# Whole first loads, a cut-up last tile and an early output in a row-wise cosine similarity

The chip is one Trainium2; the kernel runs on one of its cores. The metric is the device time of one execution in microseconds (us), as the median over several executions. All runs told here are fast (one core, granted clock 1.0).

## The reference

```python
x, y: float32 [8192, 8192]
x_norm = np.linalg.norm(x, axis=1, keepdims=True)
y_norm = np.linalg.norm(y, axis=1, keepdims=True)
return np.sum(x * y, axis=1) / (x_norm.squeeze() * y_norm.squeeze() + 1e-8)
```

For each of 8192 rows: the product of x and y summed, and the two sums of squares. Two inputs of 268 MB each are read once; 32 KB are written.

## The kernel before

64 tiles of 128 rows. Each tile is 4 MB of x and 4 MB of y. VectorE (DVE) makes the sum of x*y in one pass over 8192 columns, ScalarE (ACT) the two sums of squares in one pass each. (In the profile's lines PE is TensorE, and SPq is the queue of SyncE, which issues the loads.) Two buffers for x, two for y. The first tile's loads are cut into four groups of 32 rows.

```python
for r in range(0, P, 32):
    nc.sync.dma_start(out=xtiles[0][r : r + 32, :], in_=xv[0, r : r + 32, :])
    nc.sync.dma_start(out=ytiles[0][r : r + 32, :], in_=yv[0, r : r + 32, :])
nc.sync.dma_start(out=xtiles[1], in_=xv[1])
nc.sync.dma_start(out=ytiles[1], in_=yv[1])
# ... (identity, accumulators)
for t in range(n_tiles):
    sx = sqpool.tile([P, n_cols], bf16, tag="sq")          # one buffer
    if t + 2 < n_tiles:
        nc.sync.dma_start(out=xtiles[t + 2], in_=xv[t + 2])
        nc.sync.dma_start(out=ytiles[t + 2], in_=yv[t + 2])
    nc.vector.tensor_tensor_reduce(out=prod_s, in0=xt, in1=yt, ..., accum_out=xy_acc[:, t : t + 1])
    nc.scalar.activation(out=sx, in_=xt, func=Square, accum_out=xx_acc[:, t : t + 1])
    nc.scalar.activation(out=sx, in_=yt, func=Square, accum_out=yy_acc[:, t : t + 1])
# the short chain, once, over all 64 columns:
# nn = xx*yy (DVE), den = sqrt(nn) (ACT), rcp = 1/den (DVE), res = xy*rcp (DVE),
# transpose (PE), copy out of PSUM (DVE), one output of 64 rows of 128 values
```

## Time and profile before

| | before |
|---|---|
| median time | 1285.09 us (4 runs, 1284.73 to 1285.24) |
| span of the profiled run | 1283.3 us |
| y of tile 0 / tile 1 / tile 62 / tile 63 has landed | 43.7 / 63.0 / 1250.1 / 1269.55 us |
| from the last landing to the end of the span | 13.75 us |

The span runs from the first instruction to the last; the measured time is 1.8 us more. Landings are read off as the moment just before the pass that waited for the load, or from the chain in order of time. The profile's own lines are in the prediction below, each with what it says.

### The profile page before, as it was taken

Reading aid. Unit: us, or ns where it says so; the run is one execution under the profiler, and the core shown is the slowest. Engines: PE = TensorE matmul, PEld = TensorE weight load, DVE = VectorE, ACT = ScalarE, POOL = GpSimd, SP = SyncE. Lnnn points to the kernel's source line nnn. Section 1 sums busy time; section 2 is a strip of 40 time slices with the busy share of each in tenths; the row PEclk is TensorE's granted clock in tenths of the full one; section 3 lists DMA queues with packets and bytes.
Section 4 is the critical chain, followed back from the end, with each engine's and each line's share of the span. In section 5 each row is a group of like instructions: output and inputs, shape, how many; then the busy total and the mean of one; then the engine's idle time right before and its main releaser. Section 6 shows DMA issues by size and latency. Waiting matters only on the chain.

```text
span 1283.3 us, 905 instructions
## 1 busy us (share of the span) xinstructions
PE 0.4 (0%) x1; PEld 0.1 (0%) x1; DVE 558.0 (43%) x132; ACT 914.9 (71%) x261; POOL 0.7 (0%) x6
## 2 busy tenths in 40 slices
PE   0000000000000000000000000000000000000000
PEld 0000000000000000000000000000000000000000
DVE  0354354354353453453443543543544534534535
ACT  0677677777767767777776776777777677777766
POOL 0000000000000000000000000000000000000000
DMA  9999999999999999999999999999999999999994
GB/s 200 355 429 437 426 440 425 432 433 429 437 426 436 429 430 434 429 437 427 436 429 430 435 428 437 427 433 432 431 435 426 437 427 432 434 430 435 426 436 206
DMA packets 18615, 536.97 MB, mean 418 GB/s; under 512 B 2160, under 2 KB 2224, under 8 KB 2224
## 3 DMA queue, kind: packets, MB, share of 16 engines
q1 hardware_dynamic: 18608, 536.91, 98.9%
q14 instruction: 7, 0.06, 0.0%
HBM read 536.87 MB, written 0.03 MB: 418 GB/s over the span
## 4 chain that ended last, share of the span: by engine, by line
DMA 76%; DVE 22%; SPq 1%; issue 1%; DVEq 0%; PE 0%; ACT 0%
DMA yt<-in_y_dram 76%; DVE prod_s L74 22%; SPq L72 1%; DVEq L74 0%; DVE xy_acc L74 0%; DVE rcp L102 0%; SPq L73 0%; PE res_t_ps L107 0%; SPq L49 0%; DVE res_t L110 0%; ACT den L100 0%; DVE res L104 0%; DVE nn L98 0%
## 5 line engine op out<-in xcount | busy, mean ns | idle before, releaser
L74 DVE CUSTOM_DVE_ANT_0 prod_s<-xt,yt 128x8192 bf16<-128x8192 f32 x64 | 556.3, 8693 | 721.6 <-DMA yt<-in_y_dram 721.6
L84 ACT ACTIVATE sx<-xt 128x8192 bf16<-128x8192 f32 x64 | 449.9, 7029 | 197.8 <-DMA xt<-in_x_dram 197.8
L90 ACT ACTIVATE sx<-yt 128x8192 bf16<-128x8192 f32 x64 | 449.9, 7030 | 163.5 <-DMA yt<-in_y_dram 163.5
L90 ACT ACTIVATION_READ_ACCUMULATOR sx<-yt 128x1 f32 x64 | 11.9, 187 | 0.0
L84 ACT ACTIVATION_READ_ACCUMULATOR sx<-xt 128x1 f32 x64 | 11.9, 186 | 0.0
L74 DVE DVE_READ_ACCUMULATOR2_ANT xy_acc<- 128x1 f32 x64 | 5.3, 83 | 0.0
L55 ACT ACT_TABLE_LOAD x1 | 1.3, 1283 | 0.7 <-PEq L127 0.7
L100 ACT ACTIVATE den<-nn 128x64 f32<-128x64 f32 x1 | 0.3, 256 | 1.8 <-DVE nn L98 1.8
L56 ACT ACT_TABLE_LOAD x1 | 1.3, 1283 | 0.0
L107 PE MATMUL res_t_ps<-ident,res 128*64 128x128 f32 x1 | 0.4, 394 | 1279.8 <-DVE res L104 1279.8
L102 DVE RECIPROCAL rcp<-den 128x64 f32<-128x64 f32 x1 | 0.6, 552 | 0.3 <-ACT den L100 0.3
L110 DVE COPY res_t<-res_t_ps 64x128 f32<-64x128 f32 x1 | 0.3, 283 | 0.6 <-PE res_t_ps L107 0.6
masks.py:199 POOL TENSOR_SCALAR_AFFINE_SELECT ident<-ident 128x128 f32<-128x128 f32 x1 | 0.3, 292 | 0.1
L107 PEld LDWEIGHTS res_t_ps<-ident,res 128*64 128x64 f32 x1 | 0.1, 129 | 1279.8 <-issue 1279.8
L104 DVE TENSOR_TENSOR res<-xy_acc,rcp 128x64 f32<-128x64 f32 x1 | 0.2, 224 | 0.0
L98 DVE TENSOR_TENSOR nn<-xx_acc,yy_acc 128x64 f32<-128x64 f32 x1 | 0.2, 221 | 0.0
L55 ACT ACTIVATE dummy<-dummy 128x1 uint32<-128x1 uint32 x1 | 0.2, 203 | 0.0
L56 ACT ACTIVATE dummy<-dummy 128x1 f32<-128x1 f32 x1 | 0.2, 203 | 0.0
masks.py:197 POOL MEMSET ident<- 128x128 f32 x1 | 0.2, 204 | 0.3 <-POOLq L127 0.3
L127 POOL MEMSET const-bfloat16-1.0<- 128x1 bf16 x1 | 0.1, 101 | 0.0
L127 POOL MEMSET const-uint8-127<- 128x1 uint8 x1 | 0.1, 101 | 0.0
L127 POOL MEMSET const-float32-0.0<- 128x1 f32 x1 | 0.1, 98 | 0.2 <-issue 0.2
(1 smaller groups left out, 0.1 us busy)
## 6 DMA issues: line engine op xcount, KB each, us to landing
xt<-in_x_dram SPq DMA_DIRECT2D x63, 4096.0 KB, 20.2
yt<-in_y_dram SPq DMA_DIRECT2D x63, 4096.0 KB, 29.5
xt<-in_x_dram SPq DMA_DIRECT2D x4, 1024.0 KB, 21.3
yt<-in_y_dram SPq DMA_DIRECT2D x4, 1024.0 KB, 25.8
out_dram<-res_t SPq DMA_DIRECT2D x1, 32.0 KB, 1.8
```

The costliest lines, as they stand in the source:

```text
L55: nc.scalar.memzero(dummy)
L56: nc.scalar.sqrt(out=dummy, in_=dummy)
L72: nc.sync.dma_start(out=xtiles[t + 2], in_=xv[t + 2])
L74: nc.vector.tensor_tensor_reduce(out=prod_s, in0=xt, in1=yt, scale=1.0, scalar=0.0, op0=mybir.AluOpType.mult, op1=mybir.AluOpType.add, acc ...
L84: nc.scalar.activation(out=sx, in_=xt, func=mybir.ActivationFunctionType.Square, accum_out=xx_acc[:, t : t + 1],)
L90: nc.scalar.activation(out=sx, in_=yt, func=mybir.ActivationFunctionType.Square, accum_out=yy_acc[:, t : t + 1],)
L98: nc.vector.tensor_tensor(out=nn, in0=xx_acc, in1=yy_acc, op=mybir.AluOpType.mult)
L100: nc.scalar.activation(out=den, in_=nn, func=mybir.ActivationFunctionType.Sqrt)
L102: nc.vector.reciprocal(out=rcp, in_=den)
L107: nc.tensor.transpose(out=res_t_ps, in_=res, identity=ident)
L110: nc.vector.tensor_copy(out=res_t, in_=res_t_ps)
L127: nc = _bacc.Bacc("TRN2", target_bir_lowering=False, num_devices=1)
```

## The change

Its visible intent is a shorter end. The last tile's loads are cut by columns, so that work on a part can start before the rest has come; tiles 0 to 62 get their short chain and output while tile 63 is still loading; and the last tile's sums are arranged so that only a square root stands between its last square and the reciprocal. Along with it, without comment, the 32-row split of the first tile's loads goes. The diff is abridged, and its comments are mine:

```diff
-    for r in range(0, P, 32):
-        nc.sync.dma_start(out=xtiles[0][r : r + 32, :], in_=xv[0, r : r + 32, :])
-        nc.sync.dma_start(out=ytiles[0][r : r + 32, :], in_=yv[0, r : r + 32, :])
+    last = n_tiles - 1
+    XB = [0, 4096, 8192]
+    YB = [0, 1664, 3328, 4992, 6656, 8192]
+    cuts = {last: (XB, YB), last - 1: ([0, n_cols], [0, n_cols // 2, n_cols])}
+    # issue_dma(t): one load for each piece of cuts, else one whole load
+    issue_dma(0)
+    issue_dma(1)
 ...
+    for t in range(n_tiles - 1):
+        if t + 2 < n_tiles:
+            issue_dma(t + 2)
+        compute_tile(t)                      # as before; y of tile 62 in two passes and a sum
+        if t == n_tiles - 2:
+            chain(columns 0 to 62)           # the short chain and an output of 63 rows
+    squares(xt, XB, xxp)                     # one ACT pass a part, each with its own partial sum
+    total(xxp, nxc, xx_acc[:, lcol], "junkx")
+    squares(yt, YB[:-1], yyp)
+    total(yyp, nyc - 1, bias, "junky", scale=xx_acc[:, lcol])   # bias = xx * (y parts so far)
+    squares(yt[:, YB[-2]:], [0, n_cols - YB[-2]], yyp[:, nyc - 1:nyc])
+    # DVE: five parts of x*y, each starting from the sum of the part before (scalar=xyp[...])
+    nc.scalar.activation(out=den[:, lcol], in_=yyp[:, nyc - 1:nyc], func=Sqrt,
+                         scale=xx_acc[:, lcol], bias=bias)
+    # reciprocal, product, transpose, copy, output of one row of 128 values
```

More of the change, by code (lines that the diff above doesn't have):

```diff
@@ L46, with issue_dma, squares, total @@
     ]
-    for r in range(0, P, 32):
-        nc.sync.dma_start(out=xtiles[0][r : r + 32, :], in_=xv[0, r : r + 32, :])
-        nc.sync.dma_start(out=ytiles[0][r : r + 32, :], in_=yv[0, r : r + 32, :])
-    nc.sync.dma_start(out=xtiles[1], in_=xv[1])
-    nc.sync.dma_start(out=ytiles[1], in_=yv[1])
+    last = n_tiles - 1
+    XB = [0, 4096, 8192]
+    YB = [0, 1664, 3328, 4992, 6656, 8192]
+    cuts = {last: (XB, YB), last - 1: ([0, n_cols], [0, n_cols // 2, n_cols])}
+    def issue_dma(t):
+        xb, yb = cuts.get(t, ([0, n_cols], [0, n_cols]))
+        for a, b in zip(xb, xb[1:]):
+            nc.sync.dma_start(out=xtiles[t][:, a:b], in_=xv[t, :, a:b])
+        for a, b in zip(yb, yb[1:]):
+            nc.sync.dma_start(out=ytiles[t][:, a:b], in_=yv[t, :, a:b])
+    def squares(src, bounds, parts):
+        for c, (a, b) in enumerate(zip(bounds, bounds[1:])):
+            nc.scalar.activation(
+                out=sq_s[:, a:b], in_=src[:, a:b],
+                func=mybir.ActivationFunctionType.Square,
+                accum_out=parts[:, c:c + 1],
+            )
+    def total(parts, n, to, name, **kw):
+        junk = finpool.tile([P, n], fp32, tag=name)
+        nc.scalar.activation(
+            out=junk, in_=parts[:, 0:n],
+            func=mybir.ActivationFunctionType.Identity, accum_out=to, **kw,
+        )
+    issue_dma(0)
+    issue_dma(1)
     dummy = finpool.tile([P, 1], fp32, tag="dummy")
@@ L65, with compute_tile @@
     prod_s = prodpool.tile([P, n_cols], bf16, tag="prod")
-    for t in range(n_tiles):
+    sq_s = sqpool.tile([P, n_cols], bf16, tag="sq")
+    res = finpool.tile([P, n_tiles], fp32, tag="res")
+    nn = finpool.tile([P, n_tiles], fp32, tag="nn")
+    den = finpool.tile([P, n_tiles], fp32, tag="den")
+    rcp = finpool.tile([P, n_tiles], fp32, tag="rcp")
+    res_t_ps = psumpool.tile([n_tiles, P], fp32, tag="res_t_ps")
+    res_t = finpool.tile([n_tiles, P], fp32, tag="res_t")
+    res_t_ps_last = psumpool.tile([1, P], fp32, tag="res_t_ps_last")
+    res_row_last = finpool.tile([1, P], fp32, tag="res_row_last")
+    out_v = out.rearrange("(t p) -> t p", p=P)
+    def compute_tile(t):
         xt = xtiles[t]
         yt = ytiles[t]
-        sx = sqpool.tile([P, n_cols], bf16, tag="sq")
-        if t + 2 < n_tiles:
-            nc.sync.dma_start(out=xtiles[t + 2], in_=xv[t + 2])
-            nc.sync.dma_start(out=ytiles[t + 2], in_=yv[t + 2])
         nc.vector.tensor_tensor_reduce(
@@ L81 @@
             op1=mybir.AluOpType.add,
-            accum_out=xy_acc[:, t : t + 1],
+            accum_out=xy_acc[:, t:t + 1],
         )
         nc.scalar.activation(
-            out=sx,
+            out=sq_s,
             in_=xt,
             func=mybir.ActivationFunctionType.Square,
-            accum_out=xx_acc[:, t : t + 1],
+            accum_out=xx_acc[:, t:t + 1],
+        )
+        if t == last - 1:
+            yyp62 = accpool.tile([P, 2], fp32, tag="yyp62")
+            squares(yt, cuts[t][1], yyp62)
+            total(yyp62, 2, yy_acc[:, t:t + 1], "junk62")
+            return
@@ L89, with chain @@
+        nc.scalar.activation(
+            out=sq_s,
+            in_=yt,
+            func=mybir.ActivationFunctionType.Square,
+            accum_out=yy_acc[:, t:t + 1],
+        )
+    def chain(cols, ps, sb, orows):
+        nc.vector.tensor_tensor(
+            out=nn[:, cols], in0=xx_acc[:, cols], in1=yy_acc[:, cols],
+            op=mybir.AluOpType.mult,
         )
         nc.scalar.activation(
-            out=sx,
-            in_=yt,
-            func=mybir.ActivationFunctionType.Square,
@@ L94 @@
-            accum_out=yy_acc[:, t : t + 1],
-        )
-    nn = finpool.tile([P, n_tiles], fp32, tag="nn")
-    nc.vector.tensor_tensor(out=nn, in0=xx_acc, in1=yy_acc, op=mybir.AluOpType.mult)
-    den = finpool.tile([P, n_tiles], fp32, tag="den")
-    nc.scalar.activation(out=den, in_=nn, func=mybir.ActivationFunctionType.Sqrt)
-    rcp = finpool.tile([P, n_tiles], fp32, tag="rcp")
-    nc.vector.reciprocal(out=rcp, in_=den)
-    res = finpool.tile([P, n_tiles], fp32, tag="res")
-    nc.vector.tensor_tensor(out=res, in0=xy_acc, in1=rcp, op=mybir.AluOpType.mult)
@@ L106 @@
-    res_t_ps = psumpool.tile([n_tiles, P], fp32, tag="res_t_ps")
-    nc.tensor.transpose(out=res_t_ps, in_=res, identity=ident)
-    res_t = finpool.tile([n_tiles, P], fp32, tag="res_t")
-    nc.vector.tensor_copy(out=res_t, in_=res_t_ps)
-    out_v = out.rearrange("(t p) -> t p", p=P)
-    nc.sync.dma_start(out=out_v, in_=res_t)
+            out=den[:, cols], in_=nn[:, cols],
+            func=mybir.ActivationFunctionType.Sqrt,
+        )
+        nc.vector.reciprocal(out=rcp[:, cols], in_=den[:, cols])
@@ new lines, in chain @@
+        nc.vector.tensor_tensor(
+            out=res[:, cols], in0=xy_acc[:, cols], in1=rcp[:, cols],
+            op=mybir.AluOpType.mult,
+        )
+        nc.tensor.transpose(out=ps, in_=res[:, cols], identity=ident)
+        nc.vector.tensor_copy(out=sb, in_=ps)
+        nc.sync.dma_start(out=out_v[orows, :], in_=sb)
+    for t in range(n_tiles - 1):
[3 more added lines that the diff above has]
+        if t == n_tiles - 2:
+            e = slice(0, last)
+            chain(e, res_t_ps[e, :], res_t[e, :], e)
@@ new lines @@
+    lcol = slice(last, last + 1)
+    xt = xtiles[last]
+    yt = ytiles[last]
+    nxc, nyc = len(XB) - 1, len(YB) - 1
+    xxp = accpool.tile([P, nxc], fp32, tag="xxp")
+    yyp = accpool.tile([P, nyc], fp32, tag="yyp")
+    xyp = accpool.tile([P, nyc], fp32, tag="xyp")
+    bias = finpool.tile([P, 1], fp32, tag="bias")
+    squares(xt, XB, xxp)
[3 more added lines that the diff above has]
+    squares(yt[:, YB[-2]:], [0, n_cols - YB[-2]], yyp[:, nyc - 1:nyc])
@@ new lines @@
+    for c, (a, b) in enumerate(zip(YB, YB[1:])):
+        nc.vector.tensor_tensor_reduce(
+            out=prod_s[:, a:b], in0=xt[:, a:b], in1=yt[:, a:b],
+            scale=1.0,
+            scalar=0.0 if c == 0 else xyp[:, c - 1:c],
+            op0=mybir.AluOpType.mult, op1=mybir.AluOpType.add,
+            accum_out=xyp[:, c:c + 1],
+        )
+    nc.scalar.activation(
+        out=den[:, lcol],
+        in_=yyp[:, nyc - 1:nyc],
+        func=mybir.ActivationFunctionType.Sqrt,
+        scale=xx_acc[:, lcol],
+        bias=bias,
+    )
@@ L116 @@
+    nc.vector.reciprocal(out=rcp[:, lcol], in_=den[:, lcol])
+    nc.vector.tensor_tensor(
+        out=res[:, lcol], in0=xyp[:, nyc - 1:nyc], in1=rcp[:, lcol],
+        op=mybir.AluOpType.mult,
+    )
+    nc.tensor.transpose(out=res_t_ps_last[0:1, :], in_=res[:, lcol], identity=ident)
+    nc.vector.tensor_copy(out=res_row_last[0:1, :], in_=res_t_ps_last[0:1, :])
+    nc.sync.dma_start(out=out_v[last:last + 1, :], in_=res_row_last[0:1, :])
 _INS = ['x', 'y']
```

## The prediction

> **What bounds the kernel now.** I read the busy table and the slices of the page first, then the stretches of the head, then the timeline of the last 30 us, then the DMA issues.
>
> Page, busy table and slices:
>
> ```profile
> PE 0.4 (0%) x1; PEld 0.1 (0%) x1; DVE 558.0 (43%) x132; ACT 914.9 (71%) x261; POOL 0.7 (0%) x6
> ...
> DMA  9999999999999999999999999999999999999994
> GB/s 200 355 429 437 426 440 425 432 433 429 437 426 436 429 430 434 429 437 427 436 429 430 435 428 437 427 433 432 431 435 426 437 427 432 434 430 435 426 436 206
> ```
>
> No engine is near full, while the DMA row is 9 from start to end. But the GB/s row shows two slices that differ: the first (32 us) moves 200 GB/s with its DMA engines just as busy as later, and the second 355. The last, with 206, holds the end, where the loads are over. Those two places are where time can be had; in between nothing can, because the input is 536.87 MB and the rate is flat at about 431.
>
> Stretches (first column the stretch in us, second its length, last column GB/s, before it the DMA share):
>
> ```profile
> 0.00:3.20 3.20, 0.00 (x0) 0.00 (x0) 0.00 (x0) 2.43 (x3) 0.70 (x6) 1.00 0.69 164
> 3.20:43.80 40.60, 0.00 (x0) 0.00 (x0) 0.00 (x0) 5.45 (x3) 0.00 (x0) 1.00 0.99 207
> 43.80:63.00 19.20, 0.00 (x0) 0.00 (x0) 8.70 (x2) 16.45 (x6) 0.00 (x0) 1.00 1.02 437
> 63.00:1269.00 1206.00, 0.00 (x0) 0.00 (x0) 539.42 (x124) 883.20 (x248) 0.00 (x0) 1.00 1.00 431
> ```
>
> Until 43.8 us, while the eight 32-row loads of the first tile are under way, the same busy DMA engines move 207 GB/s; the first whole-tile loads after them move 437. The 32-row split halves the rate of its 8.39 MB.
>
> Timeline of the end (start, duration, engine, line, work, wait before it):
>
> ```profile
> 1250.22 7.03 ACT L90 ACTIVATE sx<-yt 128x8192 bf16<-128x8192 f32 x1 [2.58 <-DMA yt<-in_y_dram]
> 1259.94 7.03 ACT L84 ACTIVATE sx<-xt 128x8192 bf16<-128x8192 f32 x1 [2.60 <-DMA xt<-in_x_dram]
> 1266.87 0.19 ACT L84 ACTIVATION_READ_ACCUMULATOR sx<-xt 128x1 f32 x1
> 1269.63 7.03 ACT L90 ACTIVATE sx<-yt 128x8192 bf16<-128x8192 f32 x1 [2.58 <-DMA yt<-in_y_dram]
> 1269.71 8.69 DVE L74 CUSTOM_DVE_ANT_0 prod_s<-xt,yt 128x8192 bf16<-128x8192 f32 x1 [10.71 <-DMA yt<-in_y_dram]
> 1278.33 0.22 DVE L98 TENSOR_TENSOR nn<-xx_acc,yy_acc 128x64 f32<-128x64 f32 x1
> 1278.58 0.26 ACT L100 ACTIVATE den<-nn 128x64 f32<-128x64 f32 x1 [1.83 <-DVE nn L98]
> 1278.87 0.55 DVE L102 RECIPROCAL rcp<-den 128x64 f32<-128x64 f32 x1 [0.32 <-ACT den L100]
> 1279.46 0.22 DVE L104 TENSOR_TENSOR res<-xy_acc,rcp 128x64 f32<-128x64 f32 x1
> 1280.26 0.28 DVE L110 COPY res_t<-res_t_ps 64x128 f32<-64x128 f32 x1 [0.58 <-PE res_t_ps L107]
> 1280.57 0.55 SPq L112 DMA_DIRECT2D out_dram<-res_t  x1
> ```
>
> The last y has landed just before 1269.6 (I take 1269.55, from the chain in order of time). Then 13.75 us pass to the end of the span at 1283.3: 8.86 until the DVE has read its 8192 columns, 4.89 for the short chain and the output. The wait of 2.6 us before every ACT pass shows that ACT keeps pace with 9.7 us per 4 MB load; ACT and DVE bind only at the end.
>
> [...]
>
> **The change, part by part.**
>
> *Head: the 32-row split goes (not the visible aim of the change).* All first loads now span 128 partitions. Before, y of tile 1 lands at 63.02 (the chain: 13.43 + 49.59). After: first issue at 0.74; a fixed latency F; two tiles at full rate. The time of one tile at full rate is (1269.55 - 63.02) / 62 = 19.46 us. F from the first quarter: its load is 7.5 us from issue to landing, and 1.049 MB at 207 GB/s take 5.07, so F = 2.45. Hence y of tile 1 lands at 0.74 + 2.45 + 38.92 = 42.1. Gain 20.9 us. It is carried on to the end undiminished, as everything after is a queue at full rate: x of tile 2 is issued when DVE is done with tile 0, 8.8 us after y of tile 0 has landed, while tile 1 still has 10.6 us to transfer. Two loads are then always in flight, as before.
>
> *Middle.* Tiles 1 to 61 are unchanged: same work, same buffers. One sq buffer outside the loop instead of one of a pool with one buffer: the same. 0.
>
> *End: the loads of tile 63 are cut* into x 2 x 4096 columns and y 4 x 1664 + 1536, and tiles 0 to 62 get their chain and output early. I count from the landing of y of tile 62 as zero (before: 1250.14, so the end of the span is +33.16). A column takes 19.46/16384 us to load: x parts land at 4.87 and 9.73, y parts at 11.7, 13.7, 15.7, 17.6, 19.46.
> DVE: tile 62 until 8.7; early chain until about 11, in gaps; each y part costs 1664/0.96 ns + 0.16 fixed (8.69 less 8192/0.96 ns) = 1.9, with its accumulator read and semaphore some 2.0, the same as the arrival. So DVE ends at 19.5 + 1.76 + about 0.3 = 21.5.
> ACT: one pass costs its columns x 0.833 plus 0.32 fixed (from start to next start 7.15 us for 8192 columns, trace at 38.89 to 46.04). The second x half lands at 9.73, start 9.81, 3.73 -> 13.54. Then ACT is behind and never waits again: four y parts of 1.71 each = 6.84; the sum of the x parts 0.35; the sum of four y parts with a pointer scale 0.5; the last y part 1.60. Total 9.29 -> 22.83. So **ACT, not DVE or the DMA, ends the tail**, 3.4 us after the last landing, because it has the 3.4 us of x half to catch up on.
> Then: sqrt with pointer scale and bias 0.45 -> 23.3; reciprocal of one column about 0.2 (0.55 for 64) -> 23.5; product 0.25 -> 23.75; transpose 0.55 with its wait -> 24.3; copy 0.3 -> 24.6; output from end of copy to end of span 2.76 as before -> 27.35.
> 33.16 - 27.35 = 5.8 us gained. The small added instructions before it (early chain, its 63-row output, the two-part sum) lie beside the loads.
>
> *Sum:* 1285.09 - 20.9 - 5.8 = **1258.4 us**, 2.1% less.
>
> **Rivals.**
> A. The head gains nothing: the slow first 44 us are a start-up effect of memory, not of the 32 rows. For it: I infer the cause from position alone, the 32-row loads and the start fall together. Against: the rate is constant at 207 over four quarters and jumps at once to 437 with the first 128-row load, no warming up[...]. Then 1285.09 - 5.8 = 1279.3.
> B. The narrow column loads run slower (rows of 6.7 and 16 KB instead of 32 KB) or the queue has gaps between them. [...] As ACT is behind anyway in y, most of this is hidden; at most 1259.
> C. The tail gains less, as ACT pays more per part: self-waits on the partial sums, an extra table load. The built program has two table loads, both at the start, as before, so no switch of 1.28 us; 0.1 us more on each of nine instructions would give 1259.3. On the other side, if ACT kept up with the loads, DVE would be last and the time 1257.
> D. Buffers: the last parts' issues wait for earlier loads to land before they may be issued. The built order shows the fourth y part waiting for x of tile 62, the fifth for the first half of y of tile 62. Both have landed well before those parts' turn (about -9.7 and -4.9 on my clock, turn at 15.7 and 17.6), so 0. Were it wrong, the queue would empty for a few us: 1261.
>
> **Range and chances.** The head term is uncertain by about 0.6 us (F was measured at half the rate), the tail by 0.8, the rate over 62 tiles by 0.3 (the four runs lie 0.5 apart); A is unlikely. 1258.4, with 1256.4 to 1260.4 for 8 in 10. The 2% line is 1259.4, only 1 us away, so: faster by over 2% 0.77, within 2% 0.22, slower 0.01.
>
> **What would show it.** Right: the first slice of GB/s near 400, the first ACT pass starting near 13 us instead of 38.89, the second y landing near 42; flat 431 in between; at the end ACT without idle time from the second x half to the last square, DVE idle a little before each of its last parts, the last square ending 3 to 3.5 us after the last landing. Wrong: the first DVE pass still near 44 us (rival A), a hole in the DMA row in the last two tiles (D), or DVE's last product ending after ACT's last square (the tail worked out wrongly).

## The result, and the profile after

| | before | after |
|---|---|---|
| median time | 1285.10 us (13 runs, 1284.73 to 1285.35) | 1256.34 us (8 runs, 1256.19 to 1256.52) |
| span of the profiled run | 1283.3 us | 1254.6 us |
| y of tile 1 has landed | 63.02 us | 42.23 us |
| from the landing of y of tile 62 to the end | 33.2 us | 25.3 us |

The ratio is 0.9776 (95% interval 0.9767 to 0.9786): faster by over 2%. A ratio is the mean time of one kernel's fast runs over that of the other's of the same rounds, so not quite the ratio of the medians. The predicted 1258.4 is 2.06 us too high, and the measured median lies 0.06 us below the range.

The slices of the changed kernel's page (busy tenths of the DMA engines, then GB/s):

```profile
DMA  9999999999999999999999999999999999999997
GB/s 401 435 435 434 434 426 429 434 435 434 434 426 430 433 434 434 434 429 427 434 434 434 433 428 429 434 434 433 434 428 429 434 433 434 433 428 427 435 429 312
```

The first slice has gone from 200 GB/s to 401, the second from 355 to 435. The DMA row could not have told: it was 9 both times. The stretches of the changed kernel (stretch, length, busy time of PE, its weight loads, DVE, ACT, POOL, clock, DMA share, GB/s):

```profile
0.00:3.00 3.00, 0.00 (x0) 0.00 (x0) 0.00 (x0) 2.23 (x3) 0.70 (x6) 1.00 0.64 175
3.00:22.00 19.00, 0.00 (x0) 0.00 (x0) 0.00 (x0) 7.86 (x4) 0.00 (x0) 1.00 0.99 426
22.00:41.00 19.00, 0.00 (x0) 0.00 (x0) 8.70 (x2) 14.25 (x4) 0.00 (x0) 1.00 0.99 429
41.00:1229.00 1188.00, 0.00 (x0) 0.00 (x0) 530.71 (x122) 871.27 (x245) 0.00 (x0) 1.00 1.00 432
```

There is no slow start: the loads run at 426 from the third microsecond on, and at 432 through the middle (431 before). The passes that waited for the first x and for y of tile 1, in the changed kernel, and the latter in the kernel before:

```profile
13.13 7.03 ACT L116 ACTIVATE sq_s<-xt 128x8192 bf16<-128x8192 f32 x1 [9.38 <-DMA xt<-in_x_dram]
...
42.39 8.69 DVE L106 CUSTOM_DVE_ANT_0 prod_s<-xt,yt 128x8192 bf16<-128x8192 f32 x1 [10.75 <-DMA yt<-in_y_dram]
```

```profile
63.19 8.69 DVE L74 CUSTOM_DVE_ANT_0 prod_s<-xt,yt 128x8192 bf16<-128x8192 f32 x1 [10.59 <-DMA yt<-in_y_dram]
```

The chain puts a landing 0.16 us before its DVE pass. So the head gave 63.02 - 42.23 = 20.8 us and the middle nothing.

The end, in the changed kernel's timeline (start, duration, engine, line, work; in brackets the idle time before it):

```profile
1229.38 8.69 DVE L106 CUSTOM_DVE_ANT_0 prod_s<-xt,yt 128x8192 bf16<-128x8192 f32 x1 [10.79 <-DMA yt<-in_y_dram]
...
1239.07 3.62 ACT L63 ACTIVATE sq_s<-xt 128x4096 bf16<-128x4096 f32 x1 [0.56 <-DMA xt<-in_x_dram]
...
1241.09 1.89 DVE L175 CUSTOM_DVE_ANT_0 prod_s<-xt,yt 128x1664 bf16<-128x1664 f32 x1 [0.83 <-DMA yt<-in_y_dram]
...
1244.44 1.58 ACT L63 ACTIVATE sq_s<-yt 128x1664 bf16<-128x1664 f32 x1
...
1245.92 0.19 ACT L63 ACTIVATION_READ_ACCUMULATOR sq_s<-yt 128x1 f32 x1
1246.01 1.57 ACT L63 ACTIVATE sq_s<-yt 128x1664 bf16<-128x1664 f32 x1
...
1249.29 0.30 ACT L71 ACTIVATE junk<-yyp,xx_acc 128x4 f32<-128x4 f32 x1
1249.29 1.82 DVE L175 CUSTOM_DVE_ANT_0 prod_s<-xt,yt,xyp 128x1536 bf16<-128x1536 f32 x1
...
1250.95 0.19 ACT L63 ACTIVATION_READ_ACCUMULATOR sq_s<-yt 128x1 f32 x1
1251.03 0.08 DVE L175 DVE_READ_ACCUMULATOR2_ANT xyp<- 128x1 f32 x1
1251.17 0.39 ACT L182 ACTIVATE den<-yyp,bias,xx_acc 128x1 f32<-128x1 f32 x1
...
1252.42 0.28 DVE L195 COPY res_row_last<-res_t_ps_last 1x128 f32<-1x128 f32 x1 [0.47 <-PE res_t_ps_last L194]
1252.72 0.26 SPq L196 DMA_DIRECT2D out_dram<-res_row_last  x1
```

Read it on the prediction's clock, whose zero is the landing of y of tile 62, here 1229.30. (The DVE pass starts 0.08 after it. Taken 0.16 before the pass, as the landings of the kernel before are, it would be 1229.22; that shifts the readings below by 0.08 and changes none of the steps.)

| step | predicted | measured |
|---|---|---|
| y of tile 62 has landed, from the span's start | 1229.2 (42.13 + 61 x 19.46) | 1229.30 |
| second half of x taken up by ACT | +9.81 | 1239.07, +9.77 |
| from there until ACT is ready for the square root | 13.02 us | 1239.07 to 1251.17, 12.10 us |
| square root, reciprocal, product, transpose, copy | 1.77 us | 1251.17 to 1252.70, 1.53 us |
| from the end of the copy to the end of the span | 2.76 us | 1252.70 to 1254.6, 1.9 us |

The differences are 0.92, 0.24 and 0.86 us, together 2.02: the whole of the error. Everything up to the second half of x of the last tile is right to 0.1 us. The two big terms, 0.92 and 0.86, are what the experiments had to explain, besides the cause of the slow head, which position alone had suggested.

### The profile page after: what moved, and what is told of

It is laid out like the page before. It is cut to its first block, busy times and chain, and to the rows that moved or that the text cites.

```text
span 1254.6 us, 936 instructions
## 1 busy us (share of the span) xinstructions
PE 0.8 (0%) x2; PEld 0.3 (0%) x2; DVE 559.5 (45%) x143; ACT 917.2 (73%) x280; POOL 0.7 (0%) x6
## 4 chain that ended last, share of the span: by engine, by line
DMA 75%; DVE 22%; SPq 1%; ACT 1%; issue 1%; DVEq 0%; PE 0%
DMA yt<-in_y_dram 74%; DVE prod_s L106 21%; DMA xt<-in_x_dram 2%; SPq L57 1%; ACT sq_s L63 1%; DVEq L106 0%; SPq L59 0%; ACT junk L71 0%; DVE xy_acc L106 0%; ACT den L182 0%; PE res_t_ps_last L194 0%; DVE res_row_last L195 0%; DVE rcp L189 0%; DVE res L190 0%
## 5 line engine op out<-in xcount | busy, mean ns | idle before, releaser
L106 DVE CUSTOM_DVE_ANT_0 prod_s<-xt,yt 128x8192 bf16<-128x8192 f32 x63 | 547.6, 8692 | 690.0 <-DMA yt<-in_y_dram 690.0
L116 ACT ACTIVATE sq_s<-xt 128x8192 bf16<-128x8192 f32 x63 | 442.8, 7029 | 170.8 <-DMA xt<-in_x_dram 170.8
L127 ACT ACTIVATE sq_s<-yt 128x8192 bf16<-128x8192 f32 x62 | 435.9, 7030 | 161.8 <-DMA yt<-in_y_dram 161.8
L63 ACT ACTIVATE sq_s<-yt 128x1664 bf16<-128x1664 f32 (+2 forms) x7 | 15.0, 2140 | 0.0
L116 ACT ACTIVATION_READ_ACCUMULATOR sq_s<-xt 128x1 f32 x63 | 11.7, 186 | 0.0
L127 ACT ACTIVATION_READ_ACCUMULATOR sq_s<-yt 128x1 f32 x62 | 11.6, 186 | 0.0
L175 DVE CUSTOM_DVE_ANT_0 prod_s<-xt,yt,xyp 128x1664 bf16<-128x1664 f32 (+1 forms) x4 | 7.7, 1919 | 0.4 <-DMA yt<-in_y_dram 0.2
L63 ACT ACTIVATE sq_s<-xt 128x4096 bf16<-128x4096 f32 x2 | 7.2, 3608 | 0.6 <-DMA xt<-in_x_dram 0.6
L63 ACT ACTIVATION_READ_ACCUMULATOR sq_s<-yt 128x1 f32 x7 | 1.3, 187 | 0.0
```

What stands on the lines that cost most here:

```text
L63: nc.scalar.activation(out=sq_s[:, a:b], in_=src[:, a:b], func=mybir.ActivationFunctionType.Square, accum_out=parts[:, c:c + 1],)
L106: nc.vector.tensor_tensor_reduce(out=prod_s, in0=xt, in1=yt, scale=1.0, scalar=0.0, op0=mybir.AluOpType.mult, op1=mybir.AluOpType.add, acc ...
L116: nc.scalar.activation(out=sq_s, in_=xt, func=mybir.ActivationFunctionType.Square, accum_out=xx_acc[:, t:t + 1],)
L127: nc.scalar.activation(out=sq_s, in_=yt, func=mybir.ActivationFunctionType.Square, accum_out=yy_acc[:, t:t + 1],)
L175: nc.vector.tensor_tensor_reduce(out=prod_s[:, a:b], in0=xt[:, a:b], in1=yt[:, a:b], scale=1.0, scalar=0.0 if c == 0 else xyp[:, c - 1:c], ...
```

## The experiments

Each number below is a median; "before" beside it is from the runs of the kernel before (1284.94 to 1285.04). The runs of 0.8 us and less are compared with the changed kernel's 1256.34. It was run at another time. Their confidence intervals against it overlap, so there I lean on the separate ranges of the single times and, above all, on the durations in the traces.

### The head alone

In the kernel before, only the first tile's loads are made whole:

```diff
-    for r in range(0, P, 32):
-        nc.sync.dma_start(out=xtiles[0][r : r + 32, :], ...)   # and y
+    nc.sync.dma_start(out=xtiles[0], in_=xv[0])
+    nc.sync.dma_start(out=ytiles[0], in_=yv[0])
```

> The kernel before with only the first tile's loads made whole (128 rows each), end unchanged. Head theory (20.8 of the 28.8 us are the head): 1264.3 us, the second landing of y near 42.2 us. If the end had given most of it: near 1277.

Measured: 1264.19 us (4 runs, 1263.84 to 1264.50), 20.8 below before's 1284.95. The head theory holds to 0.1 us.

### The end alone

The changed kernel with the old loop of 32-row loads put back in place of `issue_dma(0)`.

> The changed kernel with the 32-row loads of the first tile put back, so the change of the end alone. If the two parts add up without touching each other: 1256.3 + 20.8 = 1277.1 us, 8.0 below before. If the end needs the early start for its gain: nearer to 1285.

Measured: 1277.28 us (4 runs, 1277.21 to 1277.48), 7.7 below before. The two make 28.4 of the 28.8 us: the parts add up, apart from 0.3 us. Half of that is the reference: the runs of the kernel before were 0.15 faster in this call (1284.95, not 1285.10). In the trace of the end alone, 2.1 us pass from the last copy to the end of the span, where the changed kernel has 1.9; why is not shown. Over 70% of the gain thus comes from the lines that the change did not speak of.

### What it is about the 32-row loads

Three variants of the kernel before, each with the first tile still in pieces. Under test is whether the rate goes by which partitions one load takes. Each expectation gives first what follows if it does (over 400 GB/s for a load that spans all 128, about 207 for one of adjacent partitions), then its rival. By columns, eight loads of 1 MB as before:

```diff
-    for r in range(0, P, 32): ... xtiles[0][r : r + 32, :]
+    for c in range(0, n_cols, 2048): ... xtiles[0][:, c : c + 2048]
```

> The kernel before with the first tile still in eight loads of 1 MB, but cut by columns (128 partitions x 2048) and not by rows. [...] the first 20 us run at over 400 GB/s, 1264 to 1265.5 us. Rival (loads of 1 MB are slow by their size or number, or the start is slow): no gain over 1285.

Measured: 1264.10 us (2 runs), at 429 GB/s from 3.2 to 22 us. Neither the size of a load nor their number slowed the head.

By rows, eight loads of 32 rows as before, but every fourth partition:

```diff
-    for r in range(0, P, 32): ... xtiles[0][r : r + 32, :], in_=xv[0, r : r + 32, :]
+    for r in range(4):        ... xtiles[0][r::4, :],       in_=xv[0, r::4, :]
```

> The kernel before with the first tile still in eight loads of 32 rows, but each takes every fourth partition[...]. [...] over 400 GB/s in the first 20 us, 1264 to 1266 us. Rival (32 rows are too few for the DMA engines, wherever they land): 1285.

Measured: 1264.42 us (2 runs). So 32 rows are not too few either.

By rows, four loads of 64 adjacent rows:

```diff
-    for r in range(0, P, 32): ... xtiles[0][r : r + 32, :]
+    for r in range(0, P, 64): ... xtiles[0][r : r + 64, :]
```

> The kernel before with the first tile in four loads of 64 rows of adjacent partitions. [...] still about 207 to 215 GB/s, 1284 to 1285.5 us. Rival (the rate follows the number of rows in a load): well between, near 1275.

Measured: 1285.22 us (2 runs; before 1284.94), no gain at all, though each load has twice the rows. A stretch of the first microseconds in each, first 32 rows at every fourth partition, then 64 adjacent rows (last column GB/s):

```profile
3.20:22.00 18.80, 0.00 (x0) 0.00 (x0) 0.00 (x0) 1.94 (x3) 0.00 (x0) 1.00 0.97 418
```

```profile
3.20:43.80 40.60, 0.00 (x0) 0.00 (x0) 0.00 (x0) 7.65 (x4) 0.00 (x0) 1.00 0.98 207
```

What decides is which of the 128 rows one load takes. Spread over all of them it runs at 418 even with 32 rows; in one adjacent half it runs at 207 even with 64. Start-up (rival A of the prediction) falls too: it would have slowed all these kernels, and in the same stretch, 3.2 to 22 us, the one with whole loads runs at 425 GB/s, with column loads at 429, with every fourth partition at 418.

That it is the partitions is not shown apart from one rival, and nothing here shows what lies behind it. In every run partition p receives row p, so a load of adjacent partitions also reads one adjacent stretch of 1 or 2 MB of the input, and the fast loads read from all over the tile's 4 MB. A load of adjacent partitions from every fourth row of the input would have decided, and was not run.

### The output's 0.86 us

The changed kernel's last transpose, copy and output take all 64 columns again, and the early output is left out:

```diff
-        nc.sync.dma_start(out=out_v[orows, :], in_=sb)          # the early output
-    nc.tensor.transpose(out=res_t_ps_last[0:1, :], in_=res[:, lcol], identity=ident)
-    nc.vector.tensor_copy(out=res_row_last[0:1, :], in_=res_t_ps_last[0:1, :])
-    nc.sync.dma_start(out=out_v[last:last + 1, :], in_=res_row_last[0:1, :])
+    nc.tensor.transpose(out=res_t_ps_all, in_=res, identity=ident)
+    nc.vector.tensor_copy(out=res_t_all, in_=res_t_ps_all)
+    nc.sync.dma_start(out=out_v, in_=res_t_all)
```

> The changed kernel, but the last output is 64 rows of 512 B as in the kernel before, not one row; all else of the end stays. Theory (the output's size made 0.86 of the 2.1 us by which the prediction was too high): the issue takes 0.55 us and not 0.26, and from the end of the copy to the end of the span 2.75 us pass and not 1.9; 1257.2 us. Rival (the shorter end comes from the output path being already warm by the first output): 1.9 us stay, 1256.3.

Measured: 1257.16 us (5 runs, 1256.93 to 1257.21), 0.82 above the changed kernel; the issue takes 0.54 us and 2.74 us pass from the end of the copy, 1252.66, to the end of the span, 1255.4. But this run had changed two things. It had lost the early output as well, so it did not exclude its own rival. The next run keeps the early output beside the 64-row last one (63 rows are written twice, with the same values):

> The run with the 64-row last output had also lost the early output of 63 rows, so it left open whether the last output is short because it is one row or because an output has gone before it. Here the early output stays and the last output is 64 rows (it writes 63 of them a second time). Theory (size): issue 0.55 us, 2.75 us from the end of the copy to the end, 1257.2 us. Rival (an earlier output prepares the path): about 1.9 us, 1256.4, and an issue nearer to 0.3.

Measured: 1257.09 us (5 runs, 1257.00 to 1257.37). The end of its timeline:

```profile
1252.56 0.28 DVE L197 COPY res_t_all<-res_t_ps_all 64x128 f32<-64x128 f32 x1 [0.51 <-PE res_t_ps_all L196]
1252.87 0.55 SPq L198 DMA_DIRECT2D out_dram<-res_t_all  x1
```

The issue is 0.55 us again (one row: 0.26), and the span ends at 1255.5, 2.66 us after the copy. With the early output (2.66) or without it (2.74), 64 rows take the same: the last output is short because it is smaller, not because one went before it. Whether its rows, its bytes or the number of DMA engines that share it decide is told by neither run, and the issue time does not simply follow the size: the early output of 63 rows is issued in 0.37 us in the changed kernel (at 1240.29).

A further run leaves out the transpose and the copy and writes 128 times 4 bytes straight from the result column:

```diff
-    nc.tensor.transpose(...); nc.vector.tensor_copy(...)
-    nc.sync.dma_start(out=out_v[last:last + 1, :], in_=res_row_last[0:1, :])
+    nc.sync.dma_start(out=out_v[last].rearrange("(p o) -> p o", o=1), in_=res[:, lcol])
```

> The changed kernel without the last transpose and copy: the last output goes straight from the result column, 128 partitions of 4 bytes. It saves the 0.75 us from the product's end to the copy's end. If the cost of the output goes by the DMA engines it is spread over (as theory of the 64-row output says: 0.55 us issue, 2.75 us to the end): 2.75 us after the product, about 1256.4, no change. If it goes by bytes: 1.9 us after the product, 1255.6. If 4-byte writes are slow of themselves: over 1257.

Measured: 1261.58 us (4 runs, 1261.50 to 1261.66), 5.2 worse. The 512 bytes take 7.2 us from issue to landing; the issue itself is 0.37 us. So the third branch of the expectation holds, and the transpose, which costs 0.75 us with its copy, is well worth it. As bytes alone would have given 1255.6, bytes alone are not it.

### The 0.92 us on ACT

The prediction took 0.32 us as fixed cost of an ACT pass, read off in the loop. There both passes of a tile write the same buffer, so each waits for the one before. The lines it was read off, in the kernel before:

```profile
38.89 7.03 ACT L84 ACTIVATE sx<-xt 128x8192 bf16<-128x8192 f32 x1 [35.14 <-DMA xt<-in_x_dram]
...
45.82 0.18 ACT L84 ACTIVATION_READ_ACCUMULATOR sx<-xt 128x1 f32 x1
46.04 7.03 ACT L90 ACTIVATE sx<-yt 128x8192 bf16<-128x8192 f32 x1
```

In the changed end each part writes its own slice. The run takes that away:

```diff
-                out=sq_s[:, a:b], in_=src[:, a:b],
+                out=sq_s[:, 0:b - a], in_=src[:, a:b],
-            out=junk, in_=parts[:, 0:n],
+            out=sq_s[:, 0:n], in_=parts[:, 0:n],
```

> The changed kernel with every ACT pass of the end writing the same slice of the squares' buffer, so each waits for the pass before. Theory (a pass that waits for its own engine starts 0.13 us later, and these waits made most of the 0.32 us that the prediction took for fixed): ACT from the second x half to the last square takes 12.9 us and not 12.1, 1257.1 us. Rival (short passes cost less for another reason): 12.1 us, 1256.3.

Measured: 1257.10 us (4 runs, 1256.94 to 1257.53), 0.76 above the changed kernel. Its timeline between two parts of y, and at the end of its ACT work:

```profile
1239.33 3.62 ACT L63 ACTIVATE sq_s<-xt 128x4096 bf16<-128x4096 f32 x1 [0.57 <-DMA xt<-in_x_dram]
...
1244.89 0.19 ACT L63 ACTIVATION_READ_ACCUMULATOR sq_s<-yt 128x1 f32 x1
1245.11 1.59 ACT L63 ACTIVATE sq_s<-yt 128x1664 bf16<-128x1664 f32 x1
...
1252.29 0.39 ACT L181 ACTIVATE den<-yyp,bias,xx_acc 128x1 f32<-128x1 f32 x1
```

A pass now starts 0.22 us after the start of the accumulator's read (1244.89 to 1245.11); in the changed kernel it is 0.09 (1245.92 to 1246.01), the read and the pass overlapping. The stretch from the second half of x to the square root is 1239.33 to 1252.29, 12.96 us, where the prediction had 13.02 and the changed kernel 12.10. That is the mis-sized term, put back by one change of where the passes write.

The 0.92 us has two parts, read from start to next start in the two timelines. The six passes (second half of x, five parts of y) were predicted at 12.17 us; they take 11.62 in the changed kernel and 12.22 with the shared slice. The two sums were predicted at 0.85; they take 0.48 and 0.74. So 0.55 us was in the passes and 0.37 in the sums. Two of the six passes were not shorter than predicted, the fourth and the last part of y (1.71 and 1.59 us): what follows each of them needs its sum and waits for it in any case.

### Two tries at a better end

In the changed kernel ACT and DVE finish together, at 1251.14 and 1251.11, about 2.4 us after the last landing (estimated as 1229.30 + 19.46 = 1248.76, the loads taken at full rate). First try: the last tile's x and y loaded in turn in six pairs, so that neither engine has a backlog.

```diff
-    XB = [0, 4096, 8192]
-    YB = [0, 1664, 3328, 4992, 6656, 8192]
+    B = [0, 2048, 4096, 5632, 6912, 7680, 8192]
+    # loads x[B0:B1], y[B0:B1], x[B1:B2], y[B1:B2], ...; ACT passes in the same order
```

> A version meant to beat both: x and y of the last tile loaded in turn, in six pairs of 2048, 2048, 1536, 1280, 768, 512 columns, so that ACT and DVE have no half tile to catch up on when the last part lands. If the backlog sets the end: the last square ends about 1.4 us after the last landing and not 2.4; 1255.4 us. If the twelve narrow loads lose as much in the queue, 1256.3 or more.

Measured: 1257.09 us (4 runs, 1256.99 to 1257.15), 0.75 worse than the changed kernel: the expectation failed. Its timeline, three excerpts:

```profile
1233.64 1.89 ACT L67 ACTIVATE sq_s<-xt 128x2048 bf16<-128x2048 f32 x1
...
1243.49 0.19 ACT L67 ACTIVATION_READ_ACCUMULATOR sq_s<-xt 128x1 f32 x1
1243.71 1.48 ACT L67 ACTIVATE sq_s<-yt 128x1536 bf16<-128x1536 f32 x1
...
1250.57 0.61 ACT L67 ACTIVATE sq_s<-yt 128x512 bf16<-128x512 f32 x1
1251.09 0.19 ACT L67 ACTIVATION_READ_ACCUMULATOR sq_s<-yt 128x1 f32 x1
1251.18 0.28 ACT L75 ACTIVATE junk<-yyp,xx_acc 128x5 f32<-128x5 f32 x1
1251.37 0.19 ACT L75 ACTIVATION_READ_ACCUMULATOR junk<-yyp,xx_acc 128x1 f32 x1
1251.59 0.39 ACT L187 ACTIVATE den<-yyp,bias,xx_acc 128x1 f32<-128x1 f32 x1
```

ACT works almost without a pause from 1233.64 to 1251.59: the end is now bound by its total work since tile 62, not by when parts land. I had brought in five more passes; y's pass wrote the columns that x's pass had just written, so the wait of its own engine came back (0.22 from 1243.49 to 1243.71); and the built order put the sum of the earlier y parts behind the last pass, about 0.4 us on the path. The narrow loads were late as well: DVE, which waited for the last part of y, started it 20.09 us after it had started tile 62, and at full rate the part would have come at 19.46. As ACT was behind by then, this does not show in the time.

Second try, smaller: x in 4096, 2560, 1536 columns, y in 1216, 1344 and four of 1408.

> Second try at beating both: the changed kernel with x of the last tile in 4096, 2560, 1536 columns and y in 1216, 1344 and four of 1408. Theory (ACT comes late out of the second x half, DVE has a quarter of a microsecond fixed per part and no slack, so both must be relieved a little; more parts than that cost more than they give, as the interleaved try showed): the last product on DVE ends 21.4 us after y of tile 62 has landed and not 21.8, the last square by 21.0; 1255.6 us. If the end is bound by total work and not by when parts land: 1256.3 or more.

Measured: 1256.15 us (5 runs, 1256.08 to 1256.33). Its ratio to before is 0.9776, the same as the changed kernel's, so it is not shown to be faster, and it meets neither figure of the expectation (1255.6, or 1256.3 and more). The last product on DVE ends at 1250.86, 21.84 us after the landing of y of tile 62 (1229.02 there), not the 21.4 expected. DVE runs without a pause from the second part of y on (a part of 1664 columns takes it 2.00 us from start to start in the changed kernel, about 0.27 more than its columns at 1.042 ns each, which is the expectation's quarter of a microsecond), and that part, which my arithmetic had landing at +12.8, was there only at +13.1. Narrow loads that run a little below the full rate (rival B of the prediction) would fit, with the 0.6 us of the run before and 0.2 us for the second part of y in the changed kernel; no run isolates them, so the cause stays open.

## Why the prediction was right or wrong

- **What bounds it; where time is to be had:** right. Loads at full rate in the middle before and after (431, 432), gain only at the two ends.
- **Head, 20.9 us:** right. 20.8 in the traces (63.02 to 42.23) and 20.8 in the run with the head alone. The cause, the 32 adjacent rows and not start-up, held in three runs made to break it (429 and 418 GB/s with the rows spread over all 128, 207 with 64 adjacent ones); partitions and source rows stay unseparated. Whether loads of different adjacent rows would add up to more was not tested: the eight loads landed one after the other (x's first at 8.2 us, its last at 38.8), so two of them were hardly ever under way together. The latency of 2.45 us, estimated from the first load at half the rate, held at the full rate: 42.1 predicted, 42.23 seen.
- **Middle, 0:** right; y of tile 62 landed within 0.1 us of 42.13 + 61 x 19.46.
- **End, 5.8 us:** the mechanism was right, the size was not; the traces show 7.9. The step that failed is the sum "Total 9.29 -> 22.83" and what follows it. Its term of 0.32 us fixed for each pass was read off where passes wait for their own engine; without that wait they are 0.13 us closer. The two sums, 0.35 and 0.5 by estimate, took 0.19 and 0.29 (the pass itself 0.19 us, and 0.30 for the one that reads its scale from a tile; the square root, with scale and bias from tiles, 0.39). Together the stretch was 0.92 us shorter, 12.10 us. The run with a shared slice measures 12.96 us against the 13.02 of the prediction. The rates per column were taken without a measurement, as the profile of before has one width of pass only; the runs bear them out. DVE takes 8.692 us for 8192 columns and 1.892 for 1664 (changed kernel, no sum carried in): 1.042 ns a column (0.96 columns a ns) and 0.16 us fixed. ACT with the wait, from start to next start, takes 7.15 us for 8192 columns (kernel before) and 1.72 for 1664 (shared slice): 0.83 ns a column and 0.33 us fixed.
- **"output from end of copy to end of span 2.76 as before":** the second mis-sized term. One row of 512 B takes 1.9 us, 64 rows 2.7; the prediction had carried the old figure to an output of another size. Worth 0.86 us, shown by two runs.
- **The short chain, 1.77 us:** 1.53; each small step a little under its round figure.
- **"ACT, not DVE or the DMA, ends the tail":** true in the chain, but by 0.03 us and not by 1.3, and the last square ended about 2.4 us after the estimated last landing, not 3 to 3.5. Had ACT been a little faster still, DVE would have been last. DVE came 0.3 us later than worked out (+21.81 instead of 21.5) and waited for loads only before its first two parts, not before each.
- **Rivals:** A fell. B did not show in the time of the change, but the landings hint at it (0.2 us late in the changed kernel, 0.6 with twelve loads); its bound of 1259 was my estimate, which no run shows. C was right that self-waits matter, but as the prediction had already charged them everywhere, the error went the other way. D did not happen: no hole in the DMA row.
- **The chances:** faster by over 2% was the likeliest case and came true. The range was too narrow by 0.06 us: 0.8 us was put on the end, which was 2.0 off because both wrong terms pointed the same way.

## What to carry to other kernels

A DMA row that reads full says nothing of the rate: here it was 9 at 200 GB/s and at 401. Read GB/s beside it, and try loads that take rows from the whole of the 128, which ran here at 418 to 429 GB/s where 32 or 64 adjacent rows ran at 207. A fixed cost read off in one place carries the waits of that place (here 0.13 us of 0.32); before it is used elsewhere, look whether the new instructions wait for the same things. At an end where two engines finish together, cutting finer adds passes to both and soon costs what it gives: here six pairs took 1257.09 us, three and six parts 1256.15, the changed kernel 1256.34.
